# mLSTM states of a bidirectional hybrid layer: normalizer states as transposed rows, state matrices and output gates in one transfer per head

## The chip, the cores and the metric

The kernel runs on one core of one Trainium2 chip. The metric is the device time of one execution in microseconds (us), the median of three runs. A core has a matrix engine (PE, TensorE), a vector engine (DVE), a scalar engine (ACT), a general engine (POOL, GpSimd) and an engine that mostly issues transfers (SP, SyncE). Each engine works off its own instructions in order and waits for others by semaphores; sixteen DMA engines carry the transfers between the chip's HBM (DRAM) and its SBUF memory.

## The reference

One layer step for 128 context tokens and 256 latent tokens of width 2048: modulated RMSNorm, one input projection, two groups of heads side by side (8 gated DeltaNet heads, 4 mLSTM heads), an output projection, and a feed-forward block of width 8192. All in fp32. The change concerns the mLSTM group, in particular its states: a matrix `c` (128 x 256) and a normalizer vector `n` (128) for each of 2 directions and 4 heads.

```python
def step(carry, xs):                       # mlstm_chunked, one chunk
    c, n, m = carry
    ...
    num = iw[..., None] * einsum('bhck,bhkv->bhcv', q_i, c) + einsum('bhij,bhjv->bhiv', dw, v_i)
    den = iw * einsum('bhck,bhk->bhc', q_i, n) + sum(dw, axis=-1)
    h = num / maximum(abs(den), exp(-m_t))[..., None]
    ...
    c = dec[..., None, None] * c + einsum('bhck,bhcv->bhkv', ks, v_i)
    n = dec[..., None] * n + sum(ks, axis=-2)
    return (c, n, m_new), h
# latent tokens start from the cached states; the context tokens' final c, n, m are outputs
yb = rmsnorm(hb_f + flip(hb_b), norm_b) * sigmoid(bo)        # bo: the output gates, 1024 columns
```

## The kernel before

Tokens lie in three tiles of 128 (one of context, two of latents). The weights come from HBM as fp32, half a megabyte or a quarter at a time, into a tile `raw` with five buffers (`wchunk`, line 320); ACT rounds a chunk to the fast fp32 form (`whi`, line 332), DVE takes the rest (`wlo`, line 333), and PE multiplies three products for each (`gemm`, lines 356 to 362). Between the chunks a generator of small matmuls for the modulation vectors is fed in (`ada_steps`, `raw_ada`, `ps_ada`), which uses the same five buffers.

`phase1` computes the projections that the mLSTM needs and, with the last piece, sends the output gates through a sigmoid and stores them to a DRAM scratch, one tensor per token tile (`gbd`, line 455). Then `mlstm_head` runs four times (lines 624 to 709). A head loads its two state matrices and its two normalizers into the tile `cn`, 257 columns wide for each direction: 256 of `c` and one of `n`. So one matmul `ps_num` (line 689) of the scaled queries with `cn` gives numerator and denominator together; `ps_cn` (line 674) gives the new state in the same layout, ACT copies it to `cf` (line 676), and SP stores its 256 columns and its last column separately. The normalizer's transfers are written as columns:

```python
nc.sync.dma_start(cn[:, d, DVB:DVB + 1], S.A.state_mlstm_n[0, 0, d, h].rearrange("(p o) -> p o", o=1))   # 630
nc.sync.dma_start(S.O.n[0, 0, d, h].rearrange("(p o) -> p o", o=1), cf[:, DVB:DVB + 1])                  # 678
```

Each moves 128 values of 4 bytes, one per partition, to or from 512 contiguous bytes of HBM. At its end a head loads its gates back, one transfer per token tile (`gb`, line 707), and multiplies.

A scheduler sets the order of instructions on each engine at build time, by priority and its own estimate of when things are ready. It lets the heads' work and the first projections of the DeltaNet part (`delta_v`, `delta_qk`, also `gemm`) run interleaved, so in the trace PE alternates between `ps_g` (weights) and `ps_cn`, `ps_num` (heads). SP issues all weight loads and all transfers of the heads in one queue, in that fixed order. The transfers on SP and ACT take turns on eight semaphores, and a transfer waits, on the issuing engine, until the one before it on its semaphore has landed. Small constants are loaded by POOL's queue in `setup2`.

Of the kernel before, what the change touches and what calls it, by code (L numbers as in the profile page):

```python
# [12 lines left out]
F32 = mybir.dt.float32  # L13
# [8 lines left out]
P = 128  # L22
D = 2048
NK = D // P
NT = 3
TOK = NT * P
HA = 8
HB = 4
DVB = 256
# [79 lines left out]
def setup2(S):  # L109
    nc, A, c, cp = S.nc, S.A, S.c, S.cp  # L110
    c.cw = cp.tile([P, 24, 3], F32, name="cw")
    cwr = S.p1.tile([24, P, 3], F32, name="cwr")
    nc.gpsimd.dma_start(cwr, A.conv_w[0].rearrange("(b p) j -> b p j", p=P))
    ps = S.pm.tile([P, 512], F32, tag="m", name="ps_cw")
    for j in range(3):
        nc.tensor.transpose(ps[:, 24 * j:24 * j + 24], cwr[:, :, j], c.ident[0:24, 0:24])
    nc.vector.tensor_copy(c.cw.rearrange("p b j -> p j b"), ps[:, 0:72].rearrange("p (j b) -> p j b", j=3))
    c.na = cp.tile([P, 1], F32, name="na")
    nc.gpsimd.dma_start(c.na, A.norm_a[0].rearrange("(p o) -> p o", o=1))
    c.nb = cp.tile([P, 2], F32, name="nb")  # L120
    nc.gpsimd.dma_start(c.nb, A.norm_b[0].rearrange("(b p) -> p b", p=P))
    c.alog = cp.tile([P, 16], F32, name="alog")
    nc.gpsimd.dma_start(c.alog, A.a_log[0].rearrange("d h -> (d h)").partition_broadcast(P))
    c.gbias = cp.tile([P, 32], F32, name="gbias")
    for i, ap in enumerate((A.dt_bias, A.mlstm_fbias, A.mlstm_ibias, A.state_mlstm_m)):
        o, n = ((0, 16), (16, 8), (24, 8), (0, 8))[i]
        src = ap[0].rearrange("d h -> (d h)") if i < 3 else ap[0, 0].rearrange("d h -> (d h)")
        if i < 3:
            nc.gpsimd.dma_start(c.gbias[:, o:o + n], src.partition_broadcast(P))
        else:  # L130
            c.m0b = cp.tile([P, 8], F32, name="m0b")
            nc.gpsimd.dma_start(c.m0b, src.partition_broadcast(P))
    c.m0row = cp.tile([64, 1], F32, name="m0row")
    nc.vector.memset(c.m0row, 0.0)
    for d in range(2):
        nc.gpsimd.dma_start(c.m0row[32 * d:32 * d + 4], A.state_mlstm_m[0, 0, d].rearrange("(h o) -> h o", o=1))
# [142 lines left out]
def rstd_of(S, ss, n, inv, tag):  # L279
    nc = S.nc  # L280
    v = S.wk.tile([P, n], F32, tag=tag + "v", name=tag + "v")
    nc.vector.tensor_scalar(v, ss, inv, EPS, op0=ALU.mult, op1=ALU.add)
    r = S.wk.tile([P, n], F32, tag=tag + "r", name=tag + "r")
    nc.gpsimd.tensor_tensor(r, v, S.c.nhalf.to_broadcast([P, n]), op=ALU.pow)
    return r
# [101 lines left out]
def phase1(S):  # L387
# [21 lines left out]
    for p, (k0, kn) in enumerate(pieces):  # L409
# [46 lines left out]
        if p == 1:  # L456
            setup2(S)
# [166 lines left out]
def mlstm_head(S, h):  # L624
    nc, c, G, wk = S.nc, S.c, S.G, S.ml
    qT, kT = S.bqk[h][:, 0, :], S.bqk[h][:, 1, :]
    cn = wk.tile([P, 2, DVB + 1], F32, tag="cn", name="cn")
    for d in range(2):
        nc.sync.dma_start(cn[:, d, 0:DVB], S.A.state_mlstm_C[0, 0, d, h])
        nc.sync.dma_start(cn[:, d, DVB:DVB + 1], S.A.state_mlstm_n[0, 0, d, h].rearrange("(p o) -> p o", o=1))  # L630
    qk = wk.tile([P, 5, P], F32, tag="qk", name="qk")
    p0 = S.pm.tile([P, 512], F32, tag="m", name="ps_qk0")
    nc.tensor.matmul(p0[:, 0:P], lhsT=kT[:, 0:P], rhs=qT[:, 0:P], start=True, stop=True)
# [10 lines left out]
    for d in range(2):  # L644
        col = 32 * d + h
        dh = 4 * d + h
# [28 lines left out]
        cf = wk.tile([P, DVB + 1], F32, tag="cf", name="cf")  # L675
        nc.scalar.copy(cf, pc[:, 0:DVB + 1])
        nc.sync.dma_start(S.O.C[0, 0, d, h], cf[:, 0:DVB])
        nc.sync.dma_start(S.O.n[0, 0, d, h].rearrange("(p o) -> p o", o=1), cf[:, DVB:DVB + 1])
        for it in range(NT):
            pn = S.pm.tile([P, 512], F32, tag="m", name="ps_num")  # L680
            o = pn[:, 0:DVB + 1]
# [21 lines left out]
        nc.scalar.activation(junk, hs[t], AF.Square, accum_out=ss[:, t:t + 1])  # L703
    r = rstd_of(S, ss, NT, 1.0 / DVB, "rm")
    gb = wk.tile([P, NT, DVB], F32, tag="gb", name="gb")
    for t in range(NT):
        nc.sync.dma_start(gb[:, t, :], S.gbd[t][:, h * DVB:(h + 1) * DVB])
        nc.vector.scalar_tensor_tensor(hs[t], in0=hs[t], scalar=r[:, t:t + 1], in1=gb[:, t, :],
                                       op0=ALU.mult, op1=ALU.mult)


def split_T(S, tiles, ncol, dst):
# [494 lines left out]
def body(tc, A, O):  # L1207
    with ExitStack() as ctx:
        nc = tc.nc
        S = SimpleNamespace(nc=nc, tc=tc, A=A, O=O, todo=[], credit=0.0, rate=1.7, nraw=5, av=None)  # L1210
# [10 lines left out]
        S.pa = ent(tc.tile_pool(name="pa", bufs=1, space=PSUM))  # L1221
        S.cp.tile([P, 88], F32, name="padc")
        S.gpd = [S.drp.tile([2, D], F32, name=f"gpd{i}") for i in range(2)]
        S.gbd = [S.drp.tile([P, 1024], F32, name=f"gbd{t}") for t in range(NT)]
        with ExitStack() as mx:
            S.gp = sub(mx, "gp")
            S.yB = [S.gp.tile([P, 1024], F32, name=f"yB{t}") for t in range(NT)]
# [1 line left out]
            with ExitStack() as ms:  # L1229
                S.mp = sub(ms, "mp")  # L1230
                S.ga = sub(ms, "ga")
                with tc.tile_pool(name="p1", bufs=1, reuse_waits="tile") as S.p1:
                    with tc.tile_pool(name="tp", bufs=1, reuse_waits="tile") as S.tp:
                        setup(S)
                    phase1(S)
                S.ml = sub(ms, "ml", 2)
                for h in range(HB):
                    mlstm_head(S, h)
            S.da = sub(mx, "da", 2)
            S.dl = sub(mx, "dl", 2)  # L1240
            S.de = sub(mx, "de", 2)
# [49 lines left out]
```

## Time and profile before

| what | us |
|---|---|
| median of three runs | 2011.56 |
| the three runs | 2003.14, 2011.56, 2011.78 |
| the profiled execution | 2004.86 |
| its span | 2003.1 |
| PE busy | 1944.5 (97% of the span) |
| DVE busy | 1166.2 (58%) |
| ACT busy | 711.1 (35%) |
| POOL busy | 122.8 (6%) |

Rows of the profile name an engine, a line of the kernel, an operation and its tiles as out<-in; "x4" is a count. Times are us from the span's start. A busy time counts execution alone, not waiting. "PEclk" is the granted clock of PE as a share of its full 2.4 GHz. The rows on transfers give what the sixteen DMA engines moved (GB/s) and the share of time that packets were under way, which can exceed 1. The heads of `mlstm_head` run from 302 to 412 us.

### The profile page before, as it was taken

How to read it: one execution, taken by the hardware profiler on the slowest of the kernel's cores; microseconds unless marked ns; L12 is line 12 of the kernel's file. 1: busy time of each engine (PE TensorE's matmuls, PEld its weight loads, DVE VectorE, ACT ScalarE, POOL GpSimd, SP SyncE). 2: the span in 40 equal slices, each digit the busy share in tenths (PEclk: the TensorE clock that was granted, in tenths of full speed). 3: DMA queues.
4: the chain of work that ended last, by engine and by line, in shares of the span. 5: the costliest groups of instructions: out<-in, count | busy, mean ns of one | idle time of the engine just before them, and what ended most of it. 6: DMA issues, size and time to landing. Idle time of an engine off the chain costs nothing.

```text
span 2003.1 us, 28836 instructions
## 1 busy us (share of the span) xinstructions
PE 1944.5 (97%) x11332; PEld 1673.4 (84%) x11332; DVE 1166.2 (58%) x2144; ACT 711.1 (35%) x1125; POOL 122.8 (6%) x125
## 2 busy tenths in 40 slices
PE   5999997999999999998999999999999999999997
PEld 4677886788888777787998898998989989989886
DVE  3766874668878766767455455556543443343445
ACT  5222243544344334335433342332332423323322
POOL 2000000010000000000100010000000100000002
PEclk9999998999999999998999999999999999999999
DMA  9988438776576566762454554545544344444452
GB/s 271 297 263 261 127 117 167 171 198 192 162 200 188 154 189 201 269 220 64 127 178 158 158 160 147 172 162 158 163 136 130 122 135 126 126 128 127 131 172 105
DMA packets 232356, 337.25 MB, mean 168 GB/s; under 512 B 46272, under 2 KB 115584, under 8 KB 231196
## 3 DMA queue, kind: packets, MB, share of 16 engines
q1 hardware_dynamic: 214120, 333.15, 55.1%
q10 hardware_dynamic: 17620, 2.11, 0.7%
q8 instruction: 89, 1.46, 0.3%
q14 instruction: 47, 0.39, 0.1%
q0 software_dynamic: 480, 0.15, 0.0%
HBM read 326.80 MB, written 8.56 MB: 167 GB/s over the span
## 4 chain that ended last, share of the span: by engine, by line
PE 89%; DMA 5%; DVE 4%; ACT 1%; issue 1%; POOL 0%; SPq 0%; ACTq 0%; DVEq 0%; POOLq 0%
PE ps_g L356 13%; PE ps_g L358 13%; PE ps_g L357 12%; PE ps_dn L360 8%; PE ps_dn L362 8%; PE ps_dn L361 8%; PE ps_g L360 5%; PE ps_g L362 5%; PE ps_g L361 5%; PE ps_ada L190 4%; DMA raw<-w_in 2%; DVE wlo L333 1%; PE ps_o L1027 1%; DMA raw_av<-w_ada 1%; PE ps_num L689 1%
## 5 line engine op out<-in xcount | busy, mean ns | idle before, releaser
L333 DVE TENSOR_TENSOR wlo<-raw,whi 128x1024 fp32r<-128x1024 f32 (+1 forms) x402 | 487.2, 1212 | 568.9 <-ACT whi L332 567.3
L332 ACT CAST whi<-raw 128x1024 fp32r<-128x1024 f32 (+1 forms) x402 | 417.5, 1039 | 1012.3 <-PE ps_g L357 386.8
L356 PE MATMUL ps_g<-h,whi 128*128 128x384 f32 x1536 | 522.8, 340 | 0.6 <-DVE cv L737 0.6
L358 PE MATMUL ps_g<-h,wlo 128*128 128x384 f32 x1536 | 516.3, 337 | 2.1 <-DVE wlo L333 2.1
L357 PE MATMUL ps_g<-h,whi 128*128 128x384 f32 x1536 | 517.0, 337 | 0.0
L356 PEld LDWEIGHTS ps_g<-h,whi 128*128 128x128 f32 x1536 | 288.9, 188 | 20.7 <-issue 18.7
L362 PE MATMUL ps_dn<-wlo,ah 128*128 128x512 f32 x756 | 294.5, 390 | 1.2 <-DVE wlo L333 1.2
L360 PE MATMUL ps_dn<-whi,al 128*128 128x512 f32 x756 | 294.8, 390 | 0.0
L361 PE MATMUL ps_dn<-whi,ah 128*128 128x512 f32 x756 | 294.5, 390 | 0.0
L358 PEld LDWEIGHTS ps_g<-h,wlo 128*128 128x128 f32 x1536 | 288.6, 188 | 5.1 <-DVE wlo L333 3.6
L357 PEld LDWEIGHTS ps_g<-h,whi 128*128 128x128 f32 x1536 | 288.9, 188 | 1.2 <-issue 0.7
L362 PEld LDWEIGHTS ps_dn<-wlo,ah 128*128 128x128 f32 x756 | 141.9, 188 | 31.5 <-DVE wlo L333 2.0
L360 PEld LDWEIGHTS ps_dn<-whi,al 128*128 128x128 f32 x756 | 141.9, 188 | 31.0 <-issue 1.6
L361 PEld LDWEIGHTS ps_dn<-whi,ah 128*128 128x128 f32 x756 | 141.9, 188 | 29.0
L220 DVE SCALAR_TENSOR_TENSOR adav<-raw_av,scz,adav 128x512 f32<-128x512 f32 x180 | 130.4, 773 | 12.3 <-DMA raw_av<-w_ada 12.3
L1148 POOL TENSOR_TENSOR rl<-rl 128x384 f32<-128x384 f32 x64 | 68.0, 1070 | 876.2 <-ACT ah L1147 876.0
L360 PE MATMUL ps_g<-whi,h 128*128 128x512 f32 x288 | 119.1, 413 | 1.3 <-ACT whi L332 1.2
L361 PE MATMUL ps_g<-whi,h 128*128 128x512 f32 x288 | 115.2, 400 | 0.0
L362 PE MATMUL ps_g<-wlo,h 128*128 128x512 f32 x288 | 114.2, 400 | 0.2 <-DVE wlo L333 0.2
L190 PE MATMUL ps_ada<-raw_ada,scz 128*32 128x256 f32 (+1 forms) x1216 | 100.6, 387 | 4.0 <-DMA raw_ada<-w_ada 2.6
L360 PEld LDWEIGHTS ps_g<-whi,h 128*128 128x128 f32 x288 | 54.5, 189 | 24.2 <-issue 11.7
L190 PEld LDWEIGHTS ps_ada<-raw_ada,scz 128*32 128x32 f32 x1216 | 33.9, 113 | 46.4 <-issue 27.2
(400 smaller groups left out, 1895.5 us busy)
## 6 DMA issues: line engine op xcount, KB each, us to landing
raw<-w_ffn SPq DMA_DIRECT2D x256, 512.0 KB, 3.8
raw_ada<-w_ada SPq DMA_DIRECT2D x80, 512.0 KB, 4.8
raw<-w_in SPq DMA_DIRECT2D x74, 512.0 KB, 4.7
raw_ada<-w_ada SPq DMA_DIRECT2D x128, 256.0 KB, 4.5
raw_av<-w_ada SPq DMA_DIRECT2D x48, 512.0 KB, 4.3
raw<-w_in SPq DMA_DIRECT2D x76, 256.0 KB, 3.1
raw<-w_out SPq DMA_DIRECT2D x32, 512.0 KB, 4.5
x<-x_sample SPq DMA_DIRECT2D x2, 1024.0 KB, 10.3
```

What stands on the lines that cost most here:

```text
L190: nc.tensor.matmul(ps[32 * j:32 * j + 32, 0:n], lhsT=c.scz[:, k + kk, :], rhs=raw[:, kk, u * n:u * n + n], start=k + kk < npar, stop=k + k ...
L220: nc.vector.scalar_tensor_tensor(acc[:, v, :], in0=raw[:, kt % 2, :], scalar=w, in1=acc[:, v, :], op0=ALU.mult, op1=ALU.add)
L332: nc.scalar.copy(hi, raw)
L333: nc.vector.tensor_tensor(lo, raw, hi.bitcast(F32), op=ALU.subtract)
L356: nc.tensor.matmul(o, lhsT=hi[:, kk, w], rhs=al, start=st, stop=False)
L357: nc.tensor.matmul(o, lhsT=hi[:, kk, w], rhs=ah, start=False, stop=False)
L358: nc.tensor.matmul(o, lhsT=lo[:, kk, w], rhs=ah, start=False, stop=sp)
L360: nc.tensor.matmul(o, lhsT=al[:, w], rhs=hi[:, kk, :], start=st, stop=False)
L361: nc.tensor.matmul(o, lhsT=ah[:, w], rhs=hi[:, kk, :], start=False, stop=False)
L362: nc.tensor.matmul(o, lhsT=ah[:, w], rhs=lo[:, kk, :], start=False, stop=sp)
L689: nc.tensor.matmul(o, lhsT=l, rhs=r, start=n == 0, stop=n == len(ops) - 1)
L1148: nc.gpsimd.tensor_tensor(rl, rl, rl, op=ALU.mult)
```

## The change

Four things are changed.

- The eight initial normalizers are loaded once in `setup2`, as 8 rows of 512 bytes, through POOL's queue, and transposed by PE into a tile `n0` of 128 x 8; POOL copies each head's two columns into `cn`.
- The new normalizers are copied by POOL from `cf` into the columns of a tile `n1`; after the last head `mlstm_norms` transposes it with PE, copies it to SBUF and stores 8 rows of 512 bytes in one transfer. The eight column stores on SP are gone.
- The two state matrices of a head come in one transfer.
- The scratch of the gates is one DRAM tensor, and a head loads its gates in one transfer, not three.

```diff
@@ setup2
             nc.gpsimd.dma_start(c.m0b, src.partition_broadcast(P))
+    nrow = S.p1.tile([8, P], F32, name="nrow")
+    nc.gpsimd.dma_start(nrow, A.state_mlstm_n[0, 0].rearrange("d h p -> (d h) p"))
+    ps = S.pm.tile([P, 512], F32, tag="m", name="ps_n0")
+    nc.tensor.transpose(ps[:, 0:8], nrow, c.ident[0:8, 0:8])
+    S.n0 = S.mp.tile([P, 2, HB], F32, name="n0")
+    nc.vector.tensor_copy(S.n0, ps[:, 0:8].rearrange("p (d h) -> p d h", d=2))
@@ mlstm_head
-    for d in range(2):
-        nc.sync.dma_start(cn[:, d, 0:DVB], S.A.state_mlstm_C[0, 0, d, h])
-        nc.sync.dma_start(cn[:, d, DVB:DVB + 1], S.A.state_mlstm_n[0, 0, d, h].rearrange("(p o) -> p o", o=1))
+    nc.sync.dma_start(cn[:, :, 0:DVB], S.A.state_mlstm_C[0, 0, :, h].rearrange("d p v -> p d v"))
+    nc.gpsimd.tensor_copy(cn[:, :, DVB:DVB + 1], S.n0[:, :, h:h + 1])
...
         nc.sync.dma_start(S.O.C[0, 0, d, h], cf[:, 0:DVB])
-        nc.sync.dma_start(S.O.n[0, 0, d, h].rearrange("(p o) -> p o", o=1), cf[:, DVB:DVB + 1])
+        nc.gpsimd.tensor_copy(S.n1[:, dh:dh + 1], cf[:, DVB:DVB + 1])
...
-    for t in range(NT):
-        nc.sync.dma_start(gb[:, t, :], S.gbd[t][:, h * DVB:(h + 1) * DVB])
+    nc.sync.dma_start(gb, S.gbd[:, :, h * DVB:(h + 1) * DVB].rearrange("t p v -> p t v"))
+    for t in range(NT):
         nc.vector.scalar_tensor_tensor(hs[t], in0=hs[t], scalar=r[:, t:t + 1], in1=gb[:, t, :],
                                        op0=ALU.mult, op1=ALU.mult)
+
+def mlstm_norms(S):
+    nc = S.nc
+    ps = S.pm.tile([P, 512], F32, tag="m", name="ps_n1")
+    nc.tensor.transpose(ps[0:8, 0:P], S.n1, S.c.ident)
+    row = S.ml.tile([8, P], F32, name="n1row", bufs=1)
+    nc.vector.tensor_copy(row, ps[0:8, 0:P])
+    nc.sync.dma_start(S.O.n[0, 0].rearrange("d h p -> (d h) p"), row)
@@ body
-        S.gbd = [S.drp.tile([P, 1024], F32, name=f"gbd{t}") for t in range(NT)]
+        S.gbd = S.drp.tile([NT, P, 1024], F32, name="gbd")
...
+                S.n1 = S.ml.tile([P, 8], F32, name="n1", bufs=1)
                 for h in range(HB):
                     mlstm_head(S, h)
+                mlstm_norms(S)
```

The built program has 27 transfers fewer on SP, one more on POOL, two more transposes on PE, two more copies on DVE and twelve more copies on POOL. Apart from these the order of the instructions differs in a few places only, all around the heads.

On SP, at the start of the heads, the kernel before has these rows (loads of head 1, then the stores of head 0's first direction and the next weights; `cn` are state loads, `gb` gates, `out_C` and `out_n` the stored states):

```order
L629 DMA cn<-state_mlstm_C 128x256
L630 DMA cn<-state_mlstm_n 128x1
L629 DMA cn<-state_mlstm_C 128x256
L630 DMA cn<-state_mlstm_n 128x1
L707 DMA gb<-gbd_83 128x256
L707 DMA gb<-gbd_84 128x256
L707 DMA gb<-gbd_85 128x256
L677 DMA out_C<-cf 128x256
L678 DMA out_n<-cf 128x1
L185 DMA raw_ada<-w_ada 128x1024
L328 DMA raw<-w_in 128x2x256 x2
L185 DMA raw_ada<-w_ada 128x1024
```

In the changed kernel the same place on SP, here from the loads of head 0 on, reads:

```order
L634 DMA cn<-state_mlstm_C 128x2x256
L711 DMA gb<-gbd 128x3x256
L634 DMA cn<-state_mlstm_C 128x2x256
L711 DMA gb<-gbd 128x3x256
L191 DMA raw_ada<-w_ada 128x1024
L334 DMA raw<-w_in 128x2x256 x2
L682 DMA out_C<-cf 128x256
L191 DMA raw_ada<-w_ada 128x1024
L334 DMA raw<-w_in 128x2x256 x2
L191 DMA raw_ada<-w_ada 128x1024
```

Four rows now stand where 14 were, `out_n` is gone, and one `raw_ada` and one pair of weight chunks stand ahead of the first `out_C`.

On ACT, from head 0's first `cf` to its second, the kernel before has (`yB` are the heads' results, `E`, `eM`, `ksc` the decay factors of the second direction, `whi` the cast of a weight chunk):

```order
L676 COPY cf<-ps_cn 128x257
L696 ACTIVATE yB_89<-ps_num,den 128x256
L696 ACTIVATE yB_90<-ps_num,den 128x256
L696 ACTIVATE yB_91<-ps_num,den 128x256
L656 ACTIVATE E<-E 128x512
L658 ACTIVATE eM<-ps_nm,m0b 128x256
L661 ACTIVATE ksc<-ps_nm,apad 128x1
L332 CAST whi<-raw 128x1024
L676 COPY cf<-ps_cn 128x257
```

In the changed kernel ACT has at the same place:

```order
L681 COPY cf<-ps_cn 128x257
L701 ACTIVATE yB_87<-ps_num,den 128x256
L701 ACTIVATE yB_88<-ps_num,den 128x256
L338 CAST whi<-raw 128x1024
L701 ACTIVATE yB_89<-ps_num,den 128x256
L661 ACTIVATE E<-E 128x512
L663 ACTIVATE eM<-ps_nm,m0b 128x256
L666 ACTIVATE ksc<-ps_nm,apad 128x1
L338 CAST whi<-raw 128x1024
L681 COPY cf<-ps_cn 128x257
```

The cast has moved up by four rows, ahead of the third `yB`, and the next chunk's cast has taken its old place ahead of the second `cf`.

## Rows read from the trace of the kernel before

**Rows 1.** The page, busy time (share of span) and instructions of each engine

```profile
PE 1944.5 (97%) x11332; PEld 1673.4 (84%) x11332; DVE 1166.2 (58%) x2144; ACT 711.1 (35%) x1125; POOL 122.8 (6%) x125
```

**Rows 2.** Busy time by stage; first line names the columns

```profile
core 0: us, PE busy (x) PEld busy (x) DVE busy (x) ACT busy (x) POOL busy (x), PEclk, DMA share, GB/s
296.00:412.00 116.00, 103.71 (x596) 86.25 (x595) 65.37 (x211) 55.14 (x121) 4.98 (x7) 0.96 0.81 163
412.00:700.00 288.00, 285.76 (x2330) 238.05 (x2332) 219.67 (x636) 126.12 (x293) 12.44 (x8) 1.00 0.64 186
```

**Rows 3.** The same view, parts of the heads' stage

```profile
312.00:322.00 10.00, 8.62 (x49) 6.95 (x47) 4.17 (x19) 2.75 (x7) 0.00 (x0) 1.00 0.81 40
322.00:328.00 6.00, 0.02 (x1) 0.02 (x1) 0.31 (x1) 1.32 (x2) 0.00 (x0) 0.65 0.84 299
328.00:334.00 6.00, 6.00 (x17) 5.08 (x18) 3.13 (x12) 1.96 (x8) 0.00 (x0) 0.50 1.07 55
...
340.00:348.00 8.00, 5.12 (x25) 3.18 (x24) 3.39 (x15) 2.21 (x5) 0.00 (x0) 1.00 1.13 294
...
364.00:370.00 6.00, 4.11 (x23) 2.59 (x22) 3.48 (x14) 2.74 (x5) 0.00 (x0) 1.00 0.91 290
```

**Rows 4.** Chain that ended last, its two longest waits there: start, us, what

```profile
314.39 12.12 DMA raw<-w_in
...
335.46 7.75 DMA raw<-w_in
```

**Rows 5.** Timeline of ACT and PE at the first gap: start, us, engine, line

```profile
315.44 0.47 ACT L696 ACTIVATE yB<-ps_num,den 128x256 f32<-128x256 f32 x1 [1.13 <-DVE den L694]
...
326.61 1.04 ACT L332 CAST whi<-raw 128x1024 fp32r<-128x1024 f32 x1 [9.58 <-DMA raw<-w_in]
327.56 0.37 ACT L676 COPY cf<-ps_cn 128x257 f32<-128x257 f32 x1
...
327.98 1.23 PE L689 MATMUL ps_num<-cn,qs 128*128 128x257 f32 x2 [7.36 <-ACT cf L676]
```

**Rows 6.** Timeline of SP before that gap

```profile
302.45 0.42 SPq L629 DMA_DIRECT2D cn<-state_mlstm_C  x1
...
308.54 1.38 SPq L707 DMA_DIRECT2D gb<-gbd  x3
...
312.62 0.43 SPq L678 DMA_DIRECT2D out_n<-cf  x1
...
315.46 7.32 SPq L328 DMA_DIRECT2D raw<-w_in  x1
```

**Rows 7.** Busy time again, around column loads (303), gate stores (294), column stores (others)

```profile
294.00:298.00 4.00, 4.00 (x24) 3.68 (x25) 3.50 (x10) 3.95 (x5) 0.00 (x0) 1.00 0.79 298
303.00:308.00 5.00, 5.00 (x34) 4.34 (x33) 3.26 (x9) 3.55 (x6) 0.00 (x0) 1.00 0.97 285
314.00:322.00 8.00, 6.62 (x39) 5.20 (x37) 3.09 (x13) 1.90 (x5) 0.00 (x0) 1.00 0.95 34
330.00:338.00 8.00, 8.00 (x46) 6.62 (x45) 4.76 (x15) 2.81 (x8) 0.89 (x1) 0.75 0.93 27
...
405.00:412.00 7.00, 7.00 (x52) 6.30 (x51) 4.46 (x11) 5.15 (x19) 2.39 (x4) 1.00 0.73 42
```

**Rows 8.** Transfers: out<-in, queue, count, KB each, median us from issue to landing

```profile
raw<-w_in SPq DMA_DIRECT2D x76, 256.0 KB, 3.1
...
out_delta<-Sn SPq DMA_DIRECT2D x16, 64.0 KB, 2.1
...
gpd<-grow SPq DMA_DIRECT2D x2, 16.0 KB, 1.6
```

**Rows 9.** Timeline of PE and POOL in setup, and POOL's small operations in the heads

```profile
19.62 1.68 POOL L136 DMA_DIRECT2D m0row<-state_mlstm_m  x2
...
52.14 0.52 PE L116 MATMUL ps_cw<-ident,cwr 24*128 24x24 f32 x3
...
L284 POOL TENSOR_TENSOR rmr<-rmv,nhalf x4: 848/851/885, 334.6 to 408.3; 128x3 f32<-128x3 f32 x4
```

## The prediction

> **What bounds the kernel now.** I read the page's busy times first: PE executes 97% of the span [rows 1], so time can only come out of PE's gaps, its clock or its work. Then I cut the span into stages. The heads' stage, 296 to 412 us, is the one that the change touches, and PE is busy there for 103.71 of 116 us, while in the stage behind it it is busy for 285.76 of 288 [rows 2]. So this stage has 12.29 us of gaps, and nearly all lie in three places [rows 3]: 312 to 328 (10.00 - 8.62 and 6.00 - 0.02, together 7.36), 340 to 348 (2.88), 364 to 370 (1.89); sum 12.13. A fourth loss stands in the clock column: in 328 to 334 PE is busy for all 6.00 us at a granted 0.50, which is 1.2 instead of 2.4 GHz, after it had stood still for the gap before.
>
> Next, who ends these gaps. The chain of waits has two long pieces in the stage, 12.12 and 7.75 us, both a weight chunk on its way from HBM [rows 4]; a chunk of that size takes 3.1 us in the median [rows 8]. The timelines show how such a chunk stops PE, which doesn't need it yet: ACT is in order, its cast `whi` waits 9.58 us for the chunk, the copy `cf` stands behind it, and PE's next `ps_num` waits 7.36 us for `cf` [rows 5].
>
> Last, why the chunk is late. SP issues the first `out_n` at 312.62, and a weight load that SP starts at 315.46 holds it for 7.32 us in the issue alone [rows 6]. In 314 to 322 the DMA engines are under way for 0.95 of the time and move 34 GB/s, and after the second `out_n` (330 to 338) 27 GB/s, after the last one (405 to 412) 42 GB/s [rows 7]. That isn't what stores do in general: in 294 to 298, with 2 KB rows of the gates going out, it is 298 GB/s. Nor is it the column loads, since in 303 to 308, with head 0's and 1's normalizers coming in, it is 285 GB/s [rows 7]. So the suspect is the column store: 128 pieces of 4 bytes, all into the same 512 bytes of HBM, behind which everything else stands for some 8 us, eight times. PE shows it only three times, since the five weight buffers cover the rest.
>
> On this the Trainium skill has two rules that pull apart (DMA: Bandwidth & Descriptors). Its specifications table says that transfers below 512 B make the engine read, modify and write; the rows above agree for stores (34 and 27 GB/s), not for the loads (285). Its section "Why small descriptors are slow (HBM only)" charges a small piece with some three extra cycles and 32 bytes of metadata; by that, 128 pieces on sixteen engines would cost next to nothing, the standstill would have another cause, and the change would save only issue time; that is the first rival below, which is worked out there from rows.
>
> **The change part by part.**
>
> *The eight column stores go.* In their place stands one store of 8 rows of 512 bytes at the very end of the stage. The nearest row is the 16 KB store of 32 such rows, which lands in 1.6 us, and the 64 KB ones of 128 such rows land in 2.1 [rows 8]; nothing waits for it. So the standstills go, and with them the late chunks: 12.13 us of gaps at most, and none at least, if the store isn't the cause. I take all of it here, and what stays or comes new further down.
>
> *The clock.* Without the gap of 7.36 us there is nothing after which the clock fell. The 6.00 us of work at half the clock are 3.0 us of work at the full one, so 3.0 us come back; nothing, if a gap of like length stays.
>
> *27 issues fewer on SP.* From 302.45 to 309.92 SP issues only states and gates, 14 transfers [rows 6]; afterwards 4, at the row's 0.42 us each some 1.7 us. Besides, one `raw_ada` and one pair of chunks now stand ahead of the first `out_C`, which waits for `cf`. This pair goes out some 4 us sooner than before. I count nothing extra for it, since without a standstill the chunk would be in time either way; if the standstill stays, it is the whole gain (first rival).
>
> *The merged loads.* The same bytes, in rows of the same length. A state is issued at 302.45 and is first needed about when the first stores go out, at 312 [rows 6]. A single transfer makes the first direction wait for both matrices, at most a second chunk's time (3.1 us [rows 8]) within ten. Cost nothing; if the cover went, up to 3 us once.
>
> *Twelve copies on POOL.* POOL is busy for 4.98 of 116 us [rows 2]. Its small operation with three columns takes 0.85 us [rows 9], which bounds a copy of one or two columns; twelve would be 10 us on an idle engine, and below that bound I have no row. The first matmul with `cn` waits for the copy into it, but the two first copies need only `n0`, done since setup, and those of heads 2 and 3 only that the buffer is free, a head earlier. ACT's `cf` must now wait for POOL's copy two `cf` earlier instead of the column store's landing. Nothing is queued on POOL behind a copy but the next copies and the four `rmr`. Cost nothing; if a copy came late once, 0.85 us.
>
> *Setup.* The row load stands on POOL's queue behind the other constants, at about 19.62 us, and is transposed right after the `ps_cw` at 52.14 [rows 9]; thirty microseconds cover it, against 1.6 to 3.1 for the landings at hand [rows 8]. PE gets one transpose, and one more at the end of the heads. The three of `ps_cw` take 0.52 us, so one is 0.17, two are 0.35. The last one waits for POOL's last copy, and it stands behind six `ps_num`, which cover that.
>
> *What is late next.* ACT's order has changed against us: `whi` now stands ahead of head 0's third `yB` and another `whi` ahead of the second `cf`. So a chunk must now be there at 314.3 (the third `yB` began at 315.44 after 1.13 of waiting) and the next one at 317.0 (326.61 less 9.58) [rows 5], and the latter is issued only behind the first `out_C`, at some 313 to 314; with 3.1 us it is just in time, with more it isn't. Lower bound of this wait: 0.8% of the stage, as in the stage behind, where PE alternates in the same way and stands for 2.24 of 288 us; that is 0.9 us here. Upper bound: one whole small gap in each of the three places, 1.89 each, so 5.7. I take 1.3, nearer to the stage behind, since the heads 1 to 3 have their old order on ACT but for a cast or two.
>
> Sum: 12.13 + 3.0 - 0.35 - 1.3 = 13.5 us. Against the profiled execution's own 2004.86 that is 1991.4. The span is 2003.1, so 1.8 lie around it and stay. The median of the runs is 2011.56, 6.7 above the profiled execution, and the lowest is 2003.14; I see no row that says where the 8 us between runs are. If they are in the standstills, they go too; if not, a median may come out up to 6.7 higher, at 1998. I round up a little and say **1992**. PE is the bound behind the stage, so the gain is handed on to the end.
>
> **The rivals.**
>
> *The standstill is `out_C`'s.* It is always issued 0.4 us before `out_n`, so the trace can't part them. Then it stays, and only the earlier issue helps: the pair that ended the first gap now goes out ahead of the first `out_C`. That gap shrinks by some 4 us, and with it half of the slow clock's 3.0 us: 5.5 less, 1999. Against it: stores of 512-byte rows land in 2.1 us and gate stores run at 298 GB/s [rows 7, 8], and `out_C` has 1 KB rows.
>
> *The gain is hidden anyway.* The DeltaNet stage would have to run into its own limit, say its round trips through HBM, when it starts earlier. Then it is 2004. Against it: PE stands there for only 2.24 us, and the transfers are at 0.64 of the time [rows 2]; a stage bound by anything else would show gaps.
>
> *Slower.* The casts that moved up. If a standstill of 8 us stays, whatever its cause, ACT stops at 314.3 instead of at 317.0, so that the third `yB`, `E`, `eM` and `ksc` (317.03 - 315.44, 1.6 us) come only after the chunk, and DVE's work on them too, for which I count as much again. PE would then resume not at 327.98 but 3.2 us later, and half of that again goes to the slow clock; with 3.2 at each of the two other gaps it is 11.2 us lost, 2016. It decides as soon as that chunk lands later than 315.44, by every microsecond beyond. For it speaks the order, against it that the chunk is now issued about 4 us sooner and that the heads 1 and 2 have no such move.
>
> *More than the sum.* The standstills also delay what PE's busy time hides, and the spread between runs may be theirs: 1984.
>
> **How the numbers follow.** My forecast has 0.66 (1991 to 1998 with the spread), the first rival 0.14, hidden 0.07, slower 0.05, more 0.08. The range leaves out the slower and hidden cases and about half of the uncertain ends: 1985 to 2001. What can be told from no change is about 0.5%, 10 us, so from the median of 2011.56 faster means below 2001.5: the forecast less the few cases where the median lies high (0.62), most of the first rival (0.12) and the last (0.08) make 0.82. Same gets 0.14. Slower gets 0.04: its rival lies 0.55% above the profiled execution, just outside what counts as no change.
>
> **What would show it.** Right: no stretch below 100 GB/s with the DMA engines under way for most of the time between 302 and 412; weight loads issued in under 0.5 us each; PE busy for over 98% of the heads' stage, which ends about 13 us earlier; a granted clock of 1.00 throughout it; `whi` waiting less than 3 us in all, where the first one alone waited 9.58. Wrong: a stretch of 30 to 60 GB/s behind an `out_C`; a gap of PE behind `whi` and `cf` as before; or a stage shortened by 13 us and a span that isn't.

## The result and the profile after

The changed kernel takes 1989.72 us (median of 4 runs, 1987.53 to 1993.48), the kernel before beside it 2011.61 us (4 runs, 2003.14 to 2011.78): ratio 0.9904, 95% interval 0.9887 to 0.9921. The forecast was 1992 us with a range of 1985 to 2001. The profiled execution took 1993.48 us, its span is 1991.8, so 11.4 us less than the profiled one of before.

The page's first row and the stages, in the columns of [rows 1, 2], and then the parts of the heads' stage that [rows 3] gives for before:

```profile
PE 1944.7 (98%) x11334; PEld 1674.3 (84%) x11334; DVE 1167.4 (59%) x2146; ACT 711.4 (36%) x1125; POOL 127.2 (6%) x138
```

```profile
296.00:412.00 116.00, 115.89 (x705) 97.39 (x704) 76.19 (x244) 63.02 (x141) 11.26 (x19) 1.00 0.61 185
412.00:700.00 288.00, 282.44 (x2279) 233.28 (x2278) 217.00 (x624) 122.84 (x288) 11.28 (x6) 0.99 0.63 182
...
312.00:322.00 10.00, 10.00 (x56) 8.10 (x54) 6.90 (x24) 4.92 (x10) 1.16 (x2) 1.00 0.64 186
322.00:328.00 6.00, 6.00 (x38) 4.33 (x38) 3.83 (x14) 2.32 (x9) 0.89 (x1) 1.00 0.74 220
328.00:334.00 6.00, 6.00 (x32) 4.38 (x32) 3.84 (x15) 3.25 (x8) 0.96 (x1) 1.00 0.62 210
340.00:348.00 8.00, 7.89 (x49) 6.60 (x48) 5.85 (x19) 3.72 (x11) 1.04 (x2) 1.00 0.48 124
364.00:370.00 6.00, 6.00 (x36) 4.56 (x35) 4.61 (x20) 5.25 (x12) 0.85 (x1) 1.00 0.08 13
```

PE's busy time is the same to 0.2 us. What is gone is the standing still: 0.11 us of gaps in 296 to 412, where 12.29 were, and a granted clock of 1.00 in the whole stage, where 328 to 334 had run at 0.50. That this clock gives back some 3 us doesn't show in the total of busy times, since in this execution the granted clock from 412 to 700 is 0.99 and about as much is lost there (a rough estimate: 0.01 x 288 us); in the second execution of the change, below, PE is busy for 1942.1 us. The 13 GB/s in the last row are no standstill: the DMA engines are under way for 0.08 of that time only, they have nothing to move. The stretch to compare with [rows 7] is 312 to 322, right behind the first `out_C`: 186 GB/s, where 314 to 322 had 34.

ACT's timeline at the place where before the first gap was [rows 5]:

```profile
313.30 1.03 ACT L338 CAST whi<-raw 128x1024 fp32r<-128x1024 f32 x1
315.76 0.48 ACT L701 ACTIVATE yB<-ps_num,den 128x256 f32<-128x256 f32 x1 [1.43 <-DVE den L699]
...
318.50 1.04 ACT L338 CAST whi<-raw 128x1024 fp32r<-128x1024 f32 x1 [1.16 <-PE ps_g L363]
```

The two casts that moved up stand where the order put them, at 313.30 ahead of the third `yB` and at 318.50 ahead of the second `cf`. The first waits for nothing, the second 1.16 us for PE; neither waits for the chunk from HBM, as the one at 326.61 did for 9.58 us. SP's timeline and the landings of 296 to 404 say why:

```profile
306.12 0.88 SPq L334 DMA_DIRECT2D raw<-w_in  x2
311.32 0.36 SPq L682 DMA_DIRECT2D out_C<-cf  x1
...
314.28 0.89 SPq L334 DMA_DIRECT2D raw<-w_in  x2
```

```profile
raw<-w_in SPq DMA_DIRECT2D x20, 256.0 KB, 4.3
...
out_C<-cf SPq DMA_DIRECT2D x8, 128.0 KB, 1.7
```

The pair of weight chunks that now stands ahead of `out_C` goes out at 306.12; before, it went out at 313.95, behind the first `out_n`. The next two chunks are issued in 0.89 us together, where one held SP for 7.32 us [rows 6], and the one `out_C` whose landing the trace gives lands in 1.7 us. POOL's new copies of a column out of `cf` (minimum, median and maximum in ns); the four copies of two columns into `cn` take 181 to 192 ns:

```profile
L683 POOL COPY n<-cf x8: 185/186/970, 311.4 to 386.1; 128x1 f32<-128x1 f32 x8
```

One measure serves for all runs below: the **heads' stretch**, from the first `cf` on ACT to the last `ps_num` on PE. In the profiled kernel before and after it is 403.53 - 311.84 = 91.69 us and 387.62 - 310.92 = 76.70 us:

```profile
311.84 0.37 ACT L676 COPY cf<-ps_cn 128x257 f32<-128x257 f32 x1 [3.96 <-PE ps_cn L674]
...
403.53 0.60 PE L689 MATMUL ps_num<-vaug,E 128*128 128x257 f32 x2
```

```profile
310.92 0.38 ACT L681 COPY cf<-ps_cn 128x257 f32<-128x257 f32 x1 [3.95 <-PE ps_cn L679]
...
387.62 0.60 PE L694 MATMUL ps_num<-vaug,E 128*128 128x257 f32 x2
```

So 15.0 us came out of the stage. The executions differ by 11.4; most of the rest went between 412 and 700, where PE now stands for 5.56 us instead of 2.24 [rows 2]. Two questions follow: is it the column store, and why is the median 22 us lower when the stage gave 15?

### The profile page after: what moved, and what is told of

The parts are those of the page before. It is cut to its first block, busy times and chain, and to the rows that moved or that the text cites. A ratio compares the mean times of both kernels' runs of the same rounds, so it can differ in the third digit from the quotient of the medians.

```text
span 1991.8 us, 28827 instructions
## 1 busy us (share of the span) xinstructions
PE 1944.7 (98%) x11334; PEld 1674.3 (84%) x11334; DVE 1167.4 (59%) x2146; ACT 711.4 (36%) x1125; POOL 127.2 (6%) x138
## 4 chain that ended last, share of the span: by engine, by line
PE 90%; DVE 4%; DMA 4%; ACT 1%; SPq 1%; issue 1%; POOL 0%; DVEq 0%; POOLq 0%; ACTq 0%
PE ps_g L362 13%; PE ps_g L364 12%; PE ps_g L363 12%; PE ps_dn L366 9%; PE ps_dn L368 8%; PE ps_dn L367 8%; PE ps_g L366 5%; PE ps_g L368 5%; PE ps_g L367 5%; PE ps_ada L196 4%; DMA raw<-w_in 2%; DVE wlo L339 1%; PE ps_num L694 1%; PE ps_o L1042 1%; PE ps_z L1008 1%
## 5 line engine op out<-in xcount | busy, mean ns | idle before, releaser
L366 PEld LDWEIGHTS ps_g<-whi,h 128*128 128x128 f32 x288 | 54.8, 190 | 23.5 <-issue 11.5
L368 PE MATMUL ps_g<-wlo,y 128*128 128x512 f32 x180 | 71.1, 395 | 1.5 <-DVE wlo L339 1.5
```

Source lines behind the costliest of these rows:

```text
L366: nc.tensor.matmul(o, lhsT=al[:, w], rhs=hi[:, kk, :], start=st, stop=False)
L368: nc.tensor.matmul(o, lhsT=ah[:, w], rhs=lo[:, kk, :], start=False, stop=sp)
```

## Experiments

**1. Which part of the change.** Three kernels, each the kernel before with one part, and the whole change again.

```
e1_store_rows   - nc.sync.dma_start(S.O.n[0, 0, d, h]..., cf[:, DVB:DVB + 1])
                + nc.gpsimd.tensor_copy(S.n1[:, dh:dh + 1], cf[:, DVB:DVB + 1])
                + mlstm_norms(S)      (behind the four heads, as in the change)
e2_load_rows    + nrow, ps_n0, n0 in setup, as in the change
                - nc.sync.dma_start(cn[:, d, DVB:DVB + 1], ...state_mlstm_n...)
                + nc.gpsimd.tensor_copy(cn[:, :, DVB:DVB + 1], S.n0[:, :, h:h + 1])
e3_merge        - two loads of C, three of the gates per head
                + one of each, and gbd as one tensor
```

Expected of the store alone: 

> The kernel before with one part of the change: the eight column stores of the new normalizers are replaced by copies on POOL, one transpose and one store of 8 rows. Column loads, separate state loads and gate loads stay, and so does every out_C. Theory A (the column store makes the standstill): nearly the whole gain, a ratio of 0.990 to 0.993 to the kernel before; PE gaps of the heads' stage under 3 us where there were 12.3; no stretch under 100 GB/s behind an out_C. Theory B (out_C makes it): stretches of 30 to 60 GB/s stay, ratio 0.998 to 1.000. Theory C (issues saved on SP and merged loads make the gain): only 7 issues are gone, ratio 0.997 to 1.000.

Expected of the loads alone: 

> The kernel before with the other part: the initial normalizers are loaded as 8 rows, transposed by PE, and copied into cn by POOL; the column stores stay. Theory A: the three gaps and the standstills behind out_n stay, ratio 0.997 to 1.001 (8 issues fewer on SP, and the chunks a little earlier). Theory D (4-byte pieces hurt in both directions): about half of the gain, ratio 0.994 to 0.997.

Expected of the merging alone: 

> The kernel before with only the merged transfers: two state matrices in one load, three gate tiles in one load. Column loads and column stores stay. Theory A: standstills stay, ratio 0.997 to 1.001. Theory C (issues saved and merged loads make the gain): 12 of the 27 issues are gone, ratio 0.993 to 0.996.

Expected of the whole change: 

> The changed kernel once more, to see whether the DeltaNet stage gives back some of the heads' lead each time. In its first profile the heads' stage ended 16 us earlier than before, the span only 11.3. If the giving back belongs to the new order of waits, the profile again shows a lead of 16 us at 472 (first Nx) that is 11 at the end. If it is chance, the lead at the end is 13 to 18 in this profile. Ratio to the kernel before 0.988 to 0.993.

Measured against the same runs of before (2013.15 us): the store alone 1989.78 us, ratio 0.9888 (0.9870 to 0.9907); the loads alone 2009.35, 0.9982 (0.9969 to 0.9994); the merging alone 2014.84, 1.0012 (0.9999 to 1.0025); the whole change 1987.29, 0.9881 (0.9864 to 0.9899). The heads' stage of the three parts, in the columns of [rows 2]:

```profile
296.00:412.00 116.00, 115.55 (x710) 98.10 (x709) 76.77 (x246) 63.67 (x142) 10.28 (x17) 1.00 0.63 188
```

```profile
296.00:412.00 116.00, 102.23 (x554) 82.47 (x553) 61.44 (x199) 50.89 (x106) 2.96 (x5) 0.91 0.79 160
```

```profile
296.00:412.00 116.00, 96.97 (x521) 78.14 (x520) 57.51 (x185) 47.11 (x95) 2.59 (x3) 0.91 0.76 157
```

Only the first has the gaps gone; that kernel still loads the normalizers in columns and its states in single transfers. The store is the whole gain, within what these runs can tell; its ratio is even a little below the 0.990 to 0.993 that was expected of it. The interval of the loads lies just below 1, but what would make those 0.2% stands in no row. The second run of the change ends 17.5 us ahead of the profiled kernel before (span 1985.6 against 2003.1), so the 3.6 us given back behind the stage in the first one weren't of the change's making: PE stands for 2.44 us in 412 to 700 there. In that stretch it stands for 2.1 to 7.7 us in the six profiled executions below that have the column stores, and for 2.4 to 5.6 in the five that have none.

**2. What in the store: its size or where it lands.** The changed kernel with eight column stores added, into a scratch that nothing reads. In the one the 128 pieces of 4 bytes lie side by side, as in `out_n`; in the other each has 512 bytes to itself.

```
e4_cols_same_block  + nc.sync.dma_start(S.scr[dh], cf[:, DVB:DVB + 1])           scr[dh]: 128 x 1
e5_cols_apart       + nc.sync.dma_start(S.scr[dh][:, 0:1], cf[:, DVB:DVB + 1])   scr[dh]: 128 x 128
```

Expected side by side: 

> The changed kernel with the eight column stores put back, but as copies: right behind each out_C, 128 pieces of 4 bytes go from the last column of cf into 512 contiguous bytes of a scratch in HBM that nothing reads. The row store and all else stay. Theory A1 (pieces of one 512-byte block of HBM queue up behind each other) and theory A2 (any 4-byte store costs that, wherever its piece lands): the standstills are back, eight stretches of some 8 us with 25 to 60 GB/s right behind the stores while the DMA engines are under way over 90% of the time; PE loses 8 to 20 us in 296 to 412; ratio to before 0.996 to 1.003. Theory D (the standstill needed something else of the old kernel, such as the output array itself or the column loads and single loads beside it): no such stretch, ratio 0.986 to 0.993 as for the changed kernel.

Expected apart: 

> The same eight additional column stores, but every 4-byte piece goes to a 512-byte row of its own: the scratch is 128 by 128 and only its column 0 is written. Number and size of the pieces are those of the kernel before; only where they land differs. Theory A1 (one shared 512-byte block): the pieces no longer queue up, no stretch below 100 GB/s with busy DMA engines, ratio 0.986 to 0.993. Theory A2 (each small store costs that by itself): standstills of some 8 us as with the shared block, ratio 0.996 to 1.003.

Measured: side by side 2015.22 us, ratio to before 1.0002 (0.9993 to 1.0012); apart 1991.18, 0.9883 (0.9865 to 0.9900). The two profiles, the stage and a stretch behind the first such store, then the landings in the stage; side by side first:

```profile
296.00:412.00 116.00, 101.33 (x564) 81.54 (x563) 62.53 (x202) 50.97 (x109) 6.95 (x14) 0.94 0.79 158
...
312.00:320.00 8.00, 8.00 (x47) 6.58 (x45) 4.05 (x13) 3.00 (x6) 0.00 (x0) 1.00 0.99 37
```

```profile
raw<-w_in SPq DMA_DIRECT2D x16, 256.0 KB, 9.3
...
scr<-cf SPq DMA_DIRECT2D x8, 0.5 KB, 11.0
```

and apart:

```profile
296.00:412.00 116.00, 115.76 (x702) 97.28 (x701) 75.94 (x246) 61.80 (x141) 11.23 (x19) 1.00 0.62 186
...
314.00:318.00 4.00, 4.00 (x25) 3.92 (x24) 2.37 (x8) 1.88 (x5) 0.00 (x0) 1.00 0.82 268
```

```profile
raw<-w_in SPq DMA_DIRECT2D x20, 256.0 KB, 3.0
...
scr<-cf SPq DMA_DIRECT2D x8, 0.5 KB, 1.7
```

Nor are the transfers split in another way. The whole execution has as many packets of each size in the one kernel as in the other; this is the row of the side-by-side one:

```profile
DMA packets 231060, 337.26 MB, mean 167 GB/s; under 512 B 44960, under 2 KB 114288, under 8 KB 229900
```

The same number of pieces of the same size from the same column: 11.0 us to land or 1.7, 37 GB/s or 268 for everything else, the whole gain lost or nothing. (Behind the other seven side-by-side stores, windows of 6 to 8 us show 44 to 168 GB/s.) So it isn't the 4-byte store. It is many pieces close together in HBM.

The side-by-side kernel has the changed kernel's order on ACT and its early pair of chunks, and its standstills stay. So it also shows what that order is worth then. The first of the two casts finds its chunk, which went out ahead of the store, but the second one meets the standstill in its place, and the gap of PE comes at the second `cf` as it did before [rows 5]:

```profile
326.45 1.04 ACT L338 CAST whi<-raw 128x1024 fp32r<-128x1024 f32 x1 [9.82 <-DMA raw<-w_in]
```

**3. How close is too close.** One profiled execution each: in the first, the pieces get wider and lie side by side; in the other two they stay at 4 bytes and get farther apart, in one order and in the reverse.

```
e6_widths       + w = (1, 2, 8, 16, 32, 64, 128, 4)[2 * h + d]
                + nc.sync.dma_start(S.scr[2 * h + d], cf[:, 0:w])
e8_strides      + nc.sync.dma_start(S.scr[2 * h + d][:, 0:1], cf[:, DVB:DVB + 1])
                  scr: 128 x s, s = 16, 8, 4, 2, 32, 64, 1, 128
e9_strides_rev    the same, s = 128, 1, 64, 32, 2, 4, 8, 16
```

Expected of the widths: 

> The changed kernel with one additional store behind each out_C, 128 pieces of w values out of cf into a contiguous scratch, w = 1, 2, 8, 16, 32, 64, 128, 4 for the eight passes in this order (pieces of 4, 8, 32, 64, 128, 256, 512 and 16 bytes). One look at the GB/s behind each. Theory A1 (shared 512-byte block): the standstill shrinks with the number of pieces in one block, 128, 64, 16, 8, 4, 2, 1 and 32 pieces: about 8, 4, 1, 0.5, 0.25, 0.1, 0 and 2 us. Theory A2 (any store below 512 bytes reads, modifies and writes): some 8 us behind all of them down to 256 bytes, and none behind the 512-byte one.

Expected of the distances: 

> The changed kernel with one additional column store of 128 pieces of 4 bytes behind each out_C, whose pieces stand 64, 32, 16, 8, 128, 256, 4 and 512 bytes apart in HBM, in the order of the eight passes; nothing reads them. The shared-block theory with blocks of 512 bytes: 8, 16, 32, 64, 4, 2, 128 and 1 pieces meet in one block; at some 8 us for 128 that is below 1, 1, 2, 4, 0.3, 0.1, 8 and 0 us of standstill. With blocks of 64 bytes: 1, 2, 4, 8, 1, 1, 16 and 1 pieces meet, so the first, fifth, sixth and eighth pass show nothing at all and the second to fourth little to half of the 8 us. The two differ at 64 and 128 bytes apart, where only the larger block leaves a little; the total number of pieces is the same everywhere, so a theory by which the pieces themselves cost would show 8 us behind each.

Expected of the reverse order: 

> The same with the order turned round: 512, 4, 256, 128, 8, 16, 32 and 64 bytes apart for the eight passes, so that each distance meets another place of the stage with other transfers under way. The distance decides: the second pass has the standstill of some 8 us, the fifth about half of it, the first, third and fourth nothing. The place decides: the standstill is again behind the same passes as with the first order.

Measured in the first, pieces of 4, 8, 32 and 128 bytes, from 2 us behind each store on:

```profile
314.68:316.68 2.00, 2.00 (x17) 1.59 (x11) 1.99 (x7) 0.60 (x1) 0.00 (x0) 1.00 1.68 39
...
331.55:333.55 2.00, 2.00 (x7) 1.30 (x6) 0.93 (x5) 0.86 (x6) 0.00 (x0) 0.50 0.61 44
...
344.54:346.54 2.00, 2.00 (x14) 1.27 (x14) 1.40 (x6) 0.81 (x3) 0.00 (x0) 1.00 0.72 249
...
364.21:366.21 2.00, 2.00 (x15) 1.63 (x10) 1.17 (x6) 0.76 (x2) 0.00 (x0) 1.00 0.77 244
```

With 4 bytes the standstill is back (39, 23 and 23 GB/s in three windows of 2 us, one behind the other), with 8 bytes it lasts some 4 us (44 GB/s, then 133 and 239), and from 32 bytes on 249 GB/s flow. If any store below 512 bytes cost it, all of these would stand still; that theory falls. Two passes of this kind suffice to bring the heads' stretch to 398.85 - 311.87 = 86.98 us and the time to 2001.00.

The distances. In the last of the three kernels, 4 bytes apart (second pass, two windows), 8 bytes (fifth pass, two windows), 16 and 32 bytes:

```profile
323.55:325.55 2.00, 2.00 (x14) 1.00 (x13) 1.10 (x5) 1.58 (x8) 0.00 (x0) 1.00 1.24 41
325.55:327.55 2.00, 2.00 (x19) 1.41 (x19) 1.17 (x5) 0.09 (x1) 0.89 (x1) 1.00 0.51 34
...
361.20:363.20 2.00, 2.00 (x15) 1.64 (x10) 1.17 (x6) 0.76 (x2) 0.00 (x0) 1.00 1.28 200
363.20:365.20 2.00, 2.00 (x14) 2.00 (x13) 1.67 (x4) 1.85 (x5) 0.00 (x0) 1.00 0.93 55
370.83:372.83 2.00, 2.00 (x12) 1.83 (x11) 2.00 (x13) 0.61 (x2) 0.00 (x0) 1.00 0.71 259
386.69:388.69 2.00, 2.00 (x11) 1.68 (x11) 0.94 (x6) 0.95 (x2) 0.00 (x0) 1.00 0.90 307
```

and in the other order, 64 and 32 bytes apart in the first two passes, 4 bytes in the seventh:

```profile
312.98:314.98 2.00, 2.00 (x17) 1.59 (x10) 2.00 (x7) 0.60 (x1) 0.00 (x0) 1.00 0.72 241
...
322.44:324.44 2.00, 2.00 (x14) 1.00 (x14) 1.10 (x5) 1.58 (x8) 0.00 (x0) 1.00 0.81 225
...
382.62:384.62 2.00, 2.00 (x13) 2.00 (x12) 2.00 (x4) 1.45 (x5) 0.00 (x0) 1.00 0.75 104
384.62:386.62 2.00, 2.00 (x12) 1.79 (x11) 1.85 (x7) 0.83 (x2) 0.18 (x1) 1.00 1.18 86
```

The distance decides, not the place: 4 bytes apart slows everything in both orders, 8 bytes for some 2 us, 32 bytes and more not at all; 16 bytes show 259 GB/s in the one order and 2 us of 48 GB/s, at a DMA share of 0.52, in the other. The place decides what it costs. In the second pass the single standstill makes PE wait for 4.0 us, halves its clock behind (0.50 in 337.27 to 341.27) and lengthens the heads' stretch to 395.83 - 311.49 = 84.34 us (1999.02 us in all). In the seventh, in front of which the DMA engines had little left to do (a share of 0.15 in 380.62 to 382.62), it costs PE nothing that shows: the stretch is 387.76 - 310.17 = 77.59 us (1991.57 us in all), and PE's only wait in it, of 0.4 us, lies in the second pass.

Two readings of "close" were put: that pieces in one block of 512 bytes pass one after the other, or pieces in one block of 64. Where the trace gives a landing, it says a little more than the windows. In the first order, first pass (64 bytes apart) and fourth (8 bytes), and in the reverse order, fourth pass (128 bytes):

```profile
scra<-cf SPq DMA_DIRECT2D x1, 0.5 KB, 1.5
...
scrd<-cf SPq DMA_DIRECT2D x1, 0.5 KB, 4.2
```

```profile
scrd<-cf SPq DMA_DIRECT2D x1, 0.5 KB, 1.5
```

The reverse order's first pass, 512 bytes apart, lands in 1.5 us as well, and in the sixth pass 256 bytes and 16 bytes both land in 4.2. So 64 bytes show nothing of the half microsecond that blocks of 512 would add in proportion (8 of 128 pieces at 8 us), and 8 bytes add 2.7 us, more than the half microsecond of blocks of 64. Neither reading fits in proportion, on single landings; what sets the limit between 8 and 32 bytes stays open.

**4. Another queue.** The edit that one would try first: leave the column stores as they are and take them off SP's queue.

```
e10_store_on_pool   - nc.sync.dma_start(S.O.n[0, 0, d, h]..., cf[:, DVB:DVB + 1])
                    + nc.gpsimd.dma_start(S.O.n[0, 0, d, h]..., cf[:, DVB:DVB + 1])
```

Expected: 

> The kernel before with a single edit: the eight column stores are issued by POOL on its own queue instead of by SP. If the standstill is one of the DMA engines and of HBM (theory A1), it stays: 25 to 60 GB/s behind each, ratio 0.996 to 1.003; SP is not held in its issue by the store itself, but its transfers are as late as before. If it is a matter of one queue, behind whose store the queue's next transfers stand in order, then the weight loads on SP's queue pass it: ratio 0.986 to 0.992 and the gaps of the heads' stage are gone.

Measured: 2015.50 us against 2019.06 of before, ratio 0.9979 (0.9965 to 0.9993). The stage, stretches behind the first, the second and the fourth store, and the landings:

```profile
296.00:412.00 116.00, 101.36 (x548) 82.20 (x547) 61.39 (x201) 50.34 (x105) 7.21 (x11) 0.93 0.80 156
...
312.00:316.00 4.00, 4.00 (x25) 2.92 (x24) 2.33 (x13) 1.57 (x4) 0.58 (x1) 1.00 0.55 151
...
328.00:332.00 4.00, 4.00 (x29) 3.09 (x27) 1.62 (x8) 2.52 (x7) 0.66 (x1) 0.74 0.95 25
...
348.00:352.00 4.00, 4.00 (x23) 3.81 (x22) 1.32 (x6) 0.40 (x2) 0.21 (x1) 1.00 0.59 33
```

```profile
raw<-w_in SPq DMA_DIRECT2D x15, 256.0 KB, 11.2
...
out_n<-cf POOLq DMA_DIRECT2D x8, 0.5 KB, 10.0
```

The standstill stays: 25 and 33 GB/s, and 10.0 us until the store has landed. Only behind the first store does more flow, 151 and then 180 GB/s, and 103 from 320 to 324, where PE stands. The weight loads are on another queue now and are held up all the same, 11.2 us in the median to land, so it isn't the order within a queue.

**5. The change without its merged transfers.** The change with rows both ways, but two loads of C and three of the gates per head as before:

```
e7_rows_no_merge    - nc.sync.dma_start(cn[:, :, 0:DVB], ...)     + two loads, one per direction
                    - nc.sync.dma_start(gb, ...)                  + three loads, one per tile
```

Expected: 

> The changed kernel without its merged transfers: normalizers in rows on both ways, but C loaded in two transfers per head and the gates in three. If the store is the whole gain and the merging gives nothing, as its two halves by themselves said (0.989 for the store, 0.998 for the loads, 1.001 for the merging): ratio 0.985 to 0.990, PE busy for over 115.3 of 116 us in 296 to 412. If the merged transfers matter once the standstills are gone (15 issues of SP fewer): 0.990 to 0.993, and gaps of 1 to 4 us in the heads' stage.

Measured: 1992.30 us, ratio 0.9886 (0.9869 to 0.9903), PE busy for 115.88 us of the stage: the first case. Fifteen issues of SP more cost nothing that can be measured here: the merged transfers neither help nor hurt.

**6. The kernel before once more**, for the spread between its runs.

Expected: 

> The kernel before once more, unchanged, for the time that lies between its runs (2003 to 2022 us so far, where the kernels without column stores lie within 1987 to 1994). The profile shown before is of a run of 2004.86. If the spread is made by the standstills, as the prediction supposed it might be, a run of some 2010 to 2020 us shows it in the heads' stage: PE busy for 96 to 102 of the 116 us instead of 103.71, a mean granted clock of 0.91 to 0.95 instead of 0.96, and the rest of the kernel as before. If it lies elsewhere, the stage has its 12.3 us of gaps again and the surplus stands in the DeltaNet stage or behind it.

One run, 2008.37 us, 3.5 more than the profiled one of before. Its stage, and the ends of its heads' stretch:

```profile
296.00:412.00 116.00, 100.09 (x558) 81.50 (x557) 61.55 (x201) 50.45 (x109) 2.59 (x3) 0.93 0.83 158
```

```profile
309.92 0.37 ACT L676 COPY cf<-ps_cn 128x257 f32<-128x257 f32 x1 [3.96 <-PE ps_cn L674]
...
407.33 0.60 PE L689 MATMUL ps_num<-vaug,E 128*128 128x257 f32 x2
```

The run is a little below the 2010 to 2020 that the expectation spoke of; what it shows is the first case. PE is busy for 100.09 us at a clock of 0.93, and the stretch is 407.33 - 309.92 = 97.41 us, 5.7 longer than in the first profile. Here is the stretch of all profiled executions, each the difference of two such rows, beside the rest of the execution's own time:

| kernel | own time | heads' stretch | rest |
|---|---|---|---|
| before | 2004.86 | 91.69 | 1913.2 |
| before, again | 2008.37 | 97.41 | 1911.0 |
| loads alone | 2012.94 | 97.85 | 1915.1 |
| merging alone | 2020.01 | 103.20 | 1916.8 |
| column stores on POOL | 2018.57 | 98.33 | 1920.2 |
| change + columns side by side | 2015.84 | 96.78 | 1919.1 |
| change | 1993.48 | 76.70 | 1916.8 |
| change, again | 1987.29 | 76.72 | 1910.6 |
| store alone | 1989.32 | 75.82 | 1913.5 |
| change + columns apart | 1991.23 | 76.93 | 1914.3 |
| change without merging | 1993.79 | 76.29 | 1917.5 |

The first six have all eight column stores side by side, the last five none. The rest is alike in both groups (mean 1915.9 and 1914.5); the stretch is 75.8 to 76.9 without them and 91.7 to 103.2 with them. The stretch varies by 11.5 us among the six and by 1.1 among the five, the rest by 9.2 and 6.9. So the additional spread of the kernel before is most likely made in its standstills. That is shown for the six as a group; only two of them are that kernel itself, with 91.69 and 97.41 us, and the others share its kind of store. The profile that stood at the start was the mildest of the six. The middle of the six is 97.6, of the five 76.7: 20.9 us, near the 21.9 between the medians of the runs.

## Why the prediction was right, step by step

- **The bound (PE's gaps in the heads' stage).** Right: they are gone with the store, and the time with them.
- **The suspect (eight column stores).** Right. "128 pieces of 4 bytes, all into the same 512 bytes of HBM" named two things, and only the second carries it: apart, the pieces cost nothing (experiment 2). The 12.13 us taken for it were right: 12.29 became 0.11. "Some 8 us, eight times" was read from three of the eight stores [rows 7]; behind the other five, windows of 5 to 7 us show 59 to 76 GB/s and once 163, at 355 to 362, so the standstills are not all alike.
- **The clock, 3.0 us.** Right: 1.00 in all parts of the stage shown. The gaps, the clock and one transpose make 12.29 - 0.11 + 3.0 - 0.27 = 14.9 of the 15.0 us.
- **27 issues and the merged loads, nothing.** Right: 0.9886 without the merging against 0.9881 to 0.9904 with it, and 1.0012 for it alone. The pair ahead of `out_C` went out 7.8 us sooner (306.12 for 313.95), not some 4.
- **POOL's copies, nothing.** Right, the size wrong both ways: ten of the twelve take 0.19 us, not 0.85, and two take up to 0.97, above the bound that was given. Neither shows on PE.
- **Setup and the two transposes, 0.35 us.** 0.20 and 0.27, so 0.47; nothing waited for them that the trace shows.
- **What is late next, 1.3 us.** This is the term that was mis-sized. The casts did move up, but both found their chunk there, and all of PE's gaps in the stage are 0.11 us. The rate of the stage behind was no measure for it: PE's longest wait there is 1.2 us for `Am`, a small step of the DeltaNet work on DVE, which the heads' stage doesn't have. With the rest of the sum unchanged, 14.7 us stand against 15.0 measured on the stretch.
- **The median.** The prediction left open where the 8 us between runs are, and added a margin for it at the wrong end: the median lay lower, not higher, than the profile's own sum allowed. Experiment 6 puts the additional spread into the standstills, as the rival "more than the sum" supposed. That 1992 came out within 2.3 us of 1989.72 is so far partly luck: the sum from a mild execution was 1991.4, and the gain from a usual one is some 6 us larger, from a start that is as much higher.
- **The rivals.** `out_C` as the cause: fell, all eight stay and 186 GB/s flow behind the first (its landing of 1.7 us is a single value; in the kernel with the columns apart it is 4.4). Its price was wrong too: it took 5.5 us for the earlier pair, but with that pair early and the standstills kept, side by side in experiment 2, the time is 1.0002 of before, since the next chunk takes its place in the standstill. Hidden in the DeltaNet stage: in the first run 3.6 us looked like it, in the second nothing, so it fell. Slower through the moved casts: in the change its condition, a standstill that stays, didn't come about; where it does, side by side, the moved cast finds its chunk and nothing of the 11.2 us is lost.
- **The signs.** They came, two not to the letter: ACT's `whi` waits 5.0 us in 296 to 404 for PE, but never for a chunk, and one issue of two `raw_ada` holds SP for 2.76 us at 351.05.

The Trainium skill (DMA: Bandwidth & Descriptors) had been read in two ways. Its specifications table has every transfer below 512 B read, modify and write; no run separates that from the rest, but its cost isn't what was seen, since the 4-byte stores apart land in 1.7 us and the time stays at 0.9883. Its section "Why small descriptors are slow (HBM only)", with a few cycles for each piece, fits these and falls short of the ones side by side; neither rule as read gives their 11.0 us.

## What to carry to other kernels

Look at GB/s beside the share of time in which DMA engines are under way: busy engines that move 30 GB/s were here the mark of a transfer that slows all others, and the cause was what had been issued just ahead, not what waited. A column of a tile that becomes a contiguous row in HBM was such a transfer; collect the columns, transpose them on PE (0.27 us here) and store rows, for another queue didn't help. Nor did issuing one load ahead of the standstill: the next load met it. And profile a second execution of the kernel before when its runs lie 8 us apart: the stage that varies is where the gain can come out larger or smaller than the first profile says.

## What the runs showed of the hardware that was not expected

- 128 pieces of 4 bytes that land side by side land after 9.2 to 11.7 us (experiment 2), and for some 8 us of it the sixteen DMA engines move, in the clearest cases, 23 to 42 GB/s together, whichever of the two queues tried issues them; that is an estimate of 60 ns for each piece, if they pass one by one (8 us / 128), which no run shows. At 32 bytes apart or more nothing of it is left.
- Loads of such columns do no such harm: 285 GB/s around them [rows 7], and taking them away is worth 0.2% (0.1 to 0.3).
- POOL's copy of one column takes 0.18 to 0.19 us in six cases and 0.96 and 0.97 us in two.
- One standstill alone can cost 7 us or nothing that PE shows, by what is under way when it comes: 84.34 and 77.59 us of heads' stretch with the same store in the second and in the seventh pass, 76.70 without any.
